# Six PSUM banks for the u blocks, a held exponential and earlier row requests in a fused decoder block

## The chip, the cores and the metric

The kernel is one launch on one core of one Trainium2 chip. The metric is the device time of the launch in microseconds (us); lower is better. Engine names are those of the profile: PE (matmul), DVE (vector), ACT (activation), POOL (issues the indirect DMAs), SP (issues the other DMAs).

## The reference, cut to what matters

A decoder block on 512 tokens of width 1024: adaLN, windowed attention beside a short convolution, an output projection, and then PEER, in which each token takes 8 x 16 of 16384 single-neuron experts. PEER is what the change is about:

```python
vals, ids = top_k(sc, 16)                       # per head, two halves of 128 keys
cand = vals[..., 0, :, None] + vals[..., 1, None, :]
top, pos = top_k(cand, 16)
idx, g = take_along_axis(cid, pos), softmax(top)
# per chunk of 128 tokens:
a   = einsum('chkd,cd->chk', u_tab[idx], x)     # rows of u, dot with the token
out = einsum('chk,chkd->cd', g * gelu(a), v_tab[idx])
```

## The kernel before

Tokens are split. For the first 384 (three chunks, ND = 3) PEER is done densely: every expert's pre-activation is computed by matmul, multiplied by a gate matrix that is zero for experts not chosen, and multiplied with all of v. For the last chunk of 128 tokens, and for the u side of 32 of the others, rows are gathered by indirect DMA and reduced on DVE.

**u blocks.** `first()` (L609) does one of 128 u blocks: `weights_of` loads 512 KB (SP queue, five buffers), splits it into hi (ACT, L176) and lo (DVE, L177), four buffers each; `mm3` runs 24 matmuls of 352 columns into a PSUM tile `pa`; ACT applies Gelu (L621). `pa` comes from pool `psa`, which has two banks; all other PSUM tiles come from `bank()`, pool `psm`, six banks. The first 68 blocks go out to DRAM (`Ad`), the rest stay in a ring.

**Order of the work.** Two u blocks, then the lookup of the dense chunks with three blocks per step (18 in all; from the fourth step also dots of `last_dense`, each held to an earlier block by `held[0]`), then the `ijg` transposes and three blocks, then 24 gate builds. `build(bt)` makes one-hot factors on DVE (x on ACT L919, one buffer, rewritten at every even bt; A L935; B1 and B2 L939; two buffers each), 32 small matmuls `gps` into four banks, and four ACT copies into `st`; every second build stores `st` to `Gd` (L953, SP queue). Two u blocks follow each of builds 0 to 15, one each of builds 16 to 23. Nine u blocks (63 to 71) come after the last build. The dense stage follows: `gated(m)` reads Gd back (`G`, L965) and forms hi and lo weights (L971, L972, L176, L177); `second(j)` runs 18 matmuls of 512 columns into six accumulators, which hold all six banks of `psm` to the end; from j = 68 on, one u block alternates with each `second`.

**The gathered chunk.** `gathered()` (L866) is a generator; its yields are costs, and the loops draw from it until their budget `todo` is used: 2.5 per build, 2.3 per block after the builds, `PACE` per `second`. It routes heads 0 to 3 (`route`: top-k on `scg`, `lookup`, `numbers` writes row numbers `eG`), then alternates dots with the steps of heads 4 to 7. `row(k)` asks for rows up to k + 7 (`fetch`, L770, POOL); before the dense stage the rows share one tag of six buffers. When all 128 dots are done, `weights(1, Rg)` (L697) forms the softmax: DVE subtracts (L701), ACT takes the exponential (L702), DVE sums and divides (L704 to L706). Gelu of the dots and 128 axpys (L905) follow, and `finish` writes the chunk out at the end.

**Who sets the order on an engine.** The framework fixes each engine's queue when the program is built: it plays the program through with its own costs and, when an engine is free, takes the ready instruction that stands first in program order. So later work that is ready early is pulled forward as filling. On the chip each engine runs its queue strictly in that order, and an instruction that is not ready holds all behind it. `after(ins, mark)` adds a dependency on an earlier instruction and so also delays its place. `mark[0]` is the last matmul of the latest `mm3`; `ends` lists such marks per block.

Of the kernel before, what the change touches and what calls it, by code (L numbers as in the profile page):

```python
# [7 lines left out]
F32 = mybir.dt.float32  # L8
# [5 lines left out]
AF = mybir.ActivationFunctionType  # L14
# [4 lines left out]
P = 128  # L19
# [7 lines left out]
TU = TD - HT  # L27
# [8 lines left out]
RING = 3  # L36
LOOK = 3
SPILL = 68
# [3 lines left out]
AHEAD = 7  # L42
# [47 lines left out]
def body(tc, p):  # L90
    nc = tc.nc
    es = ExitStack()

    def pool(name, bufs=1, **kw):
        st = ExitStack()
        return st.enter_context(tc.tile_pool(name=name, bufs=bufs, **kw)), st
# [4 lines left out]
    psa, psa_s = pool("psa", bufs=2, space=PSUM)  # L101
# [8 lines left out]
    def bank(name):  # L110
        return psm.tile([P, 512], F32, tag="m", name=name)
# [55 lines left out]
    mark = [None]  # L167

    def after(ins, mark):

        if mark is not None:
            tc.add_manual_dep(ins.ins, mark.ins.name, mybir.DependencyInfo(
                mybir.DependencyClass.Sync, mybir.DependencyReason.DATA), reason="pace")
# [10 lines left out]
    def parts(src):  # L184

        raw = load(src)
        h = hl.tile([P, D], F32R, tag="h", bufs=4, name="hi")
        l = hl.tile([P, D], F32R, tag="l", bufs=4, name="lo")
        split(h, l, raw)
        return h, l  # L190

    def weights_of(src):

        h, l = parts(src.rearrange("p a b -> p (a b)"))
        return (lambda k: h[:, k * P:(k + 1) * P]), (lambda k: l[:, k * P:(k + 1) * P])

    def mm3(ps, w, rh, rl, ks=range(DC), k0=0, k1=DC - 1):
        wh, wl = w
        for k in ks:
            nc.tensor.matmul(ps, wh(k), rh(k), start=(k == k0), stop=False)  # L200
            nc.tensor.matmul(ps, wh(k), rl(k), start=False, stop=False)  # L201
            mark[0] = nc.tensor.matmul(ps, wl(k), rh(k), start=False, stop=(k == k1))  # L202
# [46 lines left out]
    ps = bank("ss1")  # L249
# [13 lines left out]
    def ada_rows(r):  # L263

        if r % 2 == 0:
            psr[0] = psa.tile([P, 2, 2, P], F32, tag="a", name="psr")
        ps = psr[0][:, r % 2]
        for n in range(2):
            w = load(p["adaR"][r, n].rearrange("p a b -> p (a b)"))
            for i in range(4):  # L270
                kb = 4 * n + i
                nc.tensor.matmul(ps, ccol[:, kb:kb + 1].to_broadcast([P, P]), w[:, i * 256:(i + 1) * 256],
                                 start=(kb == 0), stop=(kb == DC - 1))
        return ps
# [8 lines left out]
    for m, k in enumerate(ORDER):  # L283
        if k < DC - NR:
            ada((k, 8 + k))
        else:
            ps = ada_rows(m)
# [193 lines left out]
    for step in PLAN.split():  # L481
        n = [int(x) for x in step[1:]]
# [80 lines left out]
    h2N = pp.tile([P, D], F32, name="h2N")  # L563
# [41 lines left out]
    Ad = dp.tile([SPILL // 2, P, 2, TU], F32, name="Ad")  # L605
    ring = {}
    lead = [0]

    def first():  # L609
        j = lead[0]  # L610
        if j == NJ:
            return
        lead[0] += 1
        w = weights_of(p["uL"][j])
        ps = psa.tile([P, TU], F32, tag="a", name="pa")
        mm3(ps, w, lambda k: h2H[:, k, :], lambda k: h2L[:, k, :])
        m, i = divmod(j, 2)
        if i == 0:
            ring[m] = up.tile([P, 2, TU], F32, name="sp", bufs=3) if j < SPILL else \
                rg.tile([P, 2, TU], F32, name="ge", bufs=RING)  # L620
        nc.scalar.activation(ring[m][:, i], ps, AF.Gelu_apprx_tanh)  # L621
        if i and j < SPILL:
            nc.sync.dma_start(Ad[m], ring.pop(m))
# [70 lines left out]
                nc.vector.tensor_add(dst[:, c, hs], eq[:, :, 0, :], eq[:, :, 1, :])  # L694
                yield

    def weights(n, R):  # L697
        g = R["g"]
        v = R["v"]
        sh = [P, n, 8, 16]  # L700
        nc.vector.tensor_sub(g, v, v[:, :, :, 0:1].to_broadcast(sh))  # L701
        nc.scalar.activation(g, g, AF.Exp)  # L702
        z = rt.tile([P, n, 8], F32, tag=f"z{n}", name="z", bufs=1)
        nc.vector.reduce_sum(z, g, axis=X)  # L704
        nc.vector.reciprocal(z, z)
        nc.vector.tensor_mul(g, g, z[:, :, :, None].to_broadcast(sh))  # L706
# [41 lines left out]
    last = None  # L748
    for hp in range(16):
# [3 lines left out]
        last = now  # L753
# [16 lines left out]
    def fetch(tab, e):  # L770
        more[0] = bool(more[1]) and not more[0]
        t = more[1][0].tile([P, D], F32, name="row2", bufs=4) if more[0] else r4.tile([P, D], F32, name="row", **R4)
        d = nc.gpsimd.indirect_dma_start(out=t, out_offset=None, in_=tab,  # L773
                                         in_offset=bass.IndirectOffsetOnAxis(ap=e, axis=0))
        if len(done) > 1:
            after(d, done.pop(0))
        return t

    def dot(a, t, h):
        junk = rt.tile([P, D], BF16, name="junk", **R2)  # L780
        return nc.vector.scalar_tensor_tensor(junk, t, 1.0, h, op0=OP.mult, op1=OP.mult, accum_out=a)  # L781

    held = [None]
# [29 lines left out]

    gN = pp.tile([P, P], F32, name="gN")
    ahead = None
    ends = []
    for n, _ in enumerate(lookup(ND, Rd)):
        if n == 1:
            ei = rt.tile([P, P], I32, tag="rest", name="ei", bufs=2)
            numbers(ei, Rd, ND - 1)  # L820
            for q in range(0, P - HT, HT):
                nc.sync.dma_start(eH[q:q + HT, :], ei[P - HT:P, q:q + HT])
            nc.vector.tensor_copy(eH[P - HT:P, :], ei[P - HT:P, P - HT:P])
            nc.vector.tensor_copy(gN, Rd["g"][:, ND - 1].rearrange("p a b -> p (a b)"))
            ahead = last_dense()
        for k in range(LOOK):
            ends.append(mark[0])
            first()
            if n > 2 and k < 2:
                held[0] = ends[-3]  # L830
                next(ahead)
    for c in range(ND):
        pt = bank("ijg")
# [10 lines left out]
        n = P if c < ND - 1 else P - HT  # L844
# [21 lines left out]
    def gathered():  # L866

        Rg = results(1, rg)
        ei = rg.tile([P, P], I32, name="eG")
        av = rg.tile([P, P], F32, name="av")  # L870
        yield from route(Rg, ei, range(0, 4))
        others = route(Rg, ei, range(4, 8))
        vR = p["vL"].rearrange("j i d -> (j i) d")
        rows = []

        def row(k, known=2 * P):

            while len(rows) < min(k + 1 + AHEAD, known):
                q, i = divmod(len(rows), P)
                rows.append(fetch(vR if q else p["uR"], ei[:, i:i + 1]))  # L880
            t, rows[k] = rows[k], None
            return t

        routed = False
        for k in range(P):
            dot(av[:, k:k + 1], row(k, 2 * P if routed else P // 2), h2N)
            yield 1.3
            if not routed:
                x = next(others, None)
                routed = x is None  # L890
                yield x or 0.0
                if k == P // 2 - 1:
                    for x in others:
                        yield x
                    routed = True
        weights(1, Rg)
        nc.scalar.activation(av, av, AF.Gelu_apprx_tanh)
        nc.vector.tensor_mul(av, av, Rg["g"].rearrange("p c a b -> p (c a b)"))
        ga = r4.tile([P, D], F32, name="ga", **R4)
        for k in range(P):  # L900
            t = row(P + k)
            if k == 0:
                nc.vector.tensor_scalar_mul(ga, t, av[:, 0:1])
            else:
                nc.vector.scalar_tensor_tensor(ga, t, av[:, k:k + 1], ga, op0=OP.mult, op1=OP.add)  # L905
            yield 1.3
        total[0] = ga
# [70 lines left out]
    def second(js, ws):  # L978

        ops = [(*w, *parts(p["vL"][j])) for j, w in zip(js, ws)]  # L980
        for c, hf in [(c, hf) for hf in range(2) for c in range(ND)] if len(js) == 1 else \
                [(c, hf) for c in range(ND) for hf in range(2)]:
            cs = slice(c * P, (c + 1) * P)
            hs = slice(hf * 512, hf * 512 + 512)
            for j, (wh, wl, vh, vl) in zip(js, ops):
                if j == 0:
                    acc[c, hf] = bank(f"o{c}{hf}")
                o = acc[c, hf]
                nc.tensor.matmul(o, wh[:, cs], vh[:, hs], start=(j == 0), stop=False)  # L989
                nc.tensor.matmul(o, wh[:, cs], vl[:, hs], start=False, stop=False)  # L990
                last = nc.tensor.matmul(o, wl[:, cs], vh[:, hs], start=False, stop=(j == NJ - 1))  # L991
        done.append(last)
        del done[:-2]

# [14 lines left out]
            nc.sync.dma_start(p["out"][c * P:(c + 1) * P, hs], x1[:, hs])  # L1009

    gb, gb_s = pool("gb")
    total = [None]
    gth = gathered()
    todo = 0.0
    nb = TD // 16
    for bt in range(nb):
# [7 lines left out]
        if not left:  # L1024
            todo += 2.5
            while todo > 0:
                todo -= next(gth)
    for k in range(SPILL + 2 * RING - 2 - lead[0]):
        first()
        todo += 2.3  # L1030
        while todo > 0:
            todo -= next(gth)
# [88 lines left out]
```

## Time and profile before

| what | us |
|---|---|
| times of three runs | 1454.32, 1452.81, 1461.66; median 1454.32 |
| the profiled execution | 1453.08, of which its span is 1451.3 |
| PE busy in the span | 1394.5 (96%) |
| DVE busy in the span | 1240.8 (85%) |
| ACT busy in the span | 616.3 (42%) |
| granted TensorE clock, mean | 0.987 |

The span runs from the first to the last instruction; 1.78 us of the profiled execution lie around it. A granted clock of 1.00 is 2.4 GHz, 0.50 is 1.2 GHz. All positions below are us from the start of the span.

### The profile page before, as it was taken

What the parts mean: (1) busy time and instruction counts of PE and PEld (TensorE: products, weight loads), DVE (VectorE), ACT (ScalarE), POOL (GpSimd) and SP (SyncE); (2) the same over time, 40 slices, a digit from 0 to 9 for tenths busy, and PEclk for the clock granted to TensorE, in tenths of its full rate; (3) what the DMA queues carried; (4) which work ended last, traced back from release to release, by engine and by line L of the source; (5) the groups of instructions that cost most, each with busy time, mean ns of one, the idle gap of its engine ahead of it and who ended that gap; (6) DMA issues with size and microseconds to landing.
All of it is one profiled execution on the core that took longest, in us unless ns stands there. A gap on an engine that the chain in (4) does not pass through costs nothing.

```text
span 1451.3 us, 21225 instructions
## 1 busy us (share of the span) xinstructions
PE 1394.5 (96%) x7696; PEld 1224.8 (84%) x7696; DVE 1240.8 (85%) x2267; ACT 616.3 (42%) x1041; POOL 405.3 (28%) x292
## 2 busy tenths in 40 slices
PE   6999998999898999798999999999999999999998
PEld 4676776788898999798988888889899999999997
DVE  7778977899999999898568888988889898889944
ACT  4524636433634556364433333433343334333431
POOL 0000000000022320511024454446646455555300
PEclk9999999999999999999999999999999999999999
DMA  7645544222586997899989999999999999999843
GB/s 276 225 158 181 194 140 170 85 96 77 176 306 239 372 381 260 309 345 343 326 301 381 401 402 373 405 344 371 341 400 360 387 352 381 386 337 402 295 130 131
DMA packets 134376, 418.80 MB, mean 289 GB/s; under 512 B 12800, under 2 KB 39552, under 8 KB 132736
## 3 DMA queue, kind: packets, MB, share of 16 engines
q1 hardware_dynamic: 92800, 266.45, 51.1%
q0 software_dynamic: 41472, 151.01, 27.5%
q8 instruction: 60, 0.98, 0.3%
q14 instruction: 44, 0.36, 0.1%
HBM read 375.77 MB, written 41.62 MB: 288 GB/s over the span
## 4 chain that ended last, share of the span: by engine, by line
PE 22%; issue 14%; POOL 8%; DMA 7%; DVE 5%; ACT 0%; POOLq 0%; DVEq 0%; ACTq 0%
POOL row L773 8%; DMA row<-in_uR,eG 5%; PE pa L200 4%; PE pa L202 4%; PE pa L201 4%; PE o L990 3%; PE o L991 3%; PE o L989 3%; DMA row<-in_vL,eG 2%; DVE lo L177 2%; DVE junk L781 1%; DVE wwl L177 0%; DVE ga L905 0%; DMA raw<-in_vL 0%; DVE x L1008 0%
## 5 line engine op out<-in xcount | busy, mean ns | idle before, releaser
L176 ACT ACTIVATE hi<-raw 128x1024 fp32r<-128x1024 f32 x298 | 312.2, 1053 | 303.2 <-PE pa L201 83.9
L177 DVE TENSOR_TENSOR lo<-raw,hi 128x1024 fp32r<-128x1024 f32 x298 | 362.4, 1217 | 49.2 <-ACT hi L176 48.7
L200 PE MATMUL pa<-h2H,hi 128*128 128x352 f32 x1024 | 336.1, 328 | 21.1 <-ACT sp L621 21.1
L202 PE MATMUL pa<-h2H,lo 128*128 128x352 f32 x1024 | 332.8, 325 | 0.4 <-DVE lo L177 0.4
L201 PE MATMUL pa<-h2L,hi 128*128 128x352 f32 x1024 | 332.0, 324 | 0.0
L989 PE MATMUL o<-hi,wwh 128*128 128x512 f32 x768 | 299.5, 390 | 0.0
L990 PE MATMUL o<-lo,wwh 128*128 128x512 f32 x768 | 299.1, 389 | 0.2 <-DVE lo L177 0.2
L991 PE MATMUL o<-hi,wwl 128*128 128x512 f32 x768 | 298.9, 389 | 0.3 <-DVE wwl L177 0.3
L773 POOL DMA_INDIRECT row<-in_uR,eG x128 | 188.9, 1476 | 326.1 <-PE o L991 165.7
L781 DVE SCALAR_TENSOR_TENSOR junk<-row,h2N 128x1024 bf16<-128x1024 f32 x128 | 153.9, 1220 | 72.9 <-DMA row<-in_uR,eG 72.7
L200 PEld LDWEIGHTS pa<-h2H,hi 128*128 128x128 f32 x1024 | 194.8, 190 | 25.1 <-ACT sp L621 22.8
L773 POOL DMA_INDIRECT row<-in_vL,eG x128 | 171.7, 1341 | 145.6 <-PE o L991 91.3
L201 PEld LDWEIGHTS pa<-h2L,hi 128*128 128x128 f32 x1024 | 195.3, 191 | 2.2
L202 PEld LDWEIGHTS pa<-h2H,lo 128*128 128x128 f32 x1024 | 195.2, 191 | 0.7 <-DVE lo L177 0.7
L905 DVE SCALAR_TENSOR_TENSOR ga<-row,av,ga 128x1024 f32<-128x1024 f32 x127 | 163.0, 1283 | 25.6 <-DMA row<-in_vL,eG 24.5
L773 POOL DMA_INDIRECT row<-in_uR,eH x32 | 44.5, 1392 | 489.3 <-ACT sp L621 394.8
L991 PEld LDWEIGHTS o<-hi,wwl 128*128 128x128 f32 x768 | 144.1, 188 | 30.9 <-DVE wwl L177 0.7
L990 PEld LDWEIGHTS o<-lo,wwh 128*128 128x128 f32 x768 | 144.2, 188 | 28.7 <-DVE lo L177 0.6
L989 PEld LDWEIGHTS o<-hi,wwh 128*128 128x128 f32 x768 | 144.2, 188 | 28.2 <-issue 0.2
L176 ACT ACTIVATE wwh<-w 128x768 fp32r<-128x768 f32 x64 | 54.1, 845 | 156.9 <-DVE w L972 123.3
L971 ACT ACTIVATE w<-G 128x32 f32<-128x32 f32 x128 | 22.3, 222 | 196.3 <-DVE wwl L177 191.6
L177 DVE TENSOR_TENSOR wwl<-w,wwh 128x768 fp32r<-128x768 f32 x64 | 60.8, 951 | 10.5 <-ACT wwh L176 10.5
(265 smaller groups left out, 1831.2 us busy)
## 6 DMA issues: line engine op xcount, KB each, us to landing
raw<-in_uL SPq DMA_DIRECT2D x128, 512.0 KB, 6.2
raw<-in_vL SPq DMA_DIRECT2D x128, 512.0 KB, 6.9
Gd<-st SPq DMA_DIRECT2D x12, 2048.0 KB, 10.4
G<-Gd SPq DMA_DIRECT2D x16, 1536.0 KB, 11.7
ada<-in_ada SPq DMA_DIRECT2D x32, 512.0 KB, 4.2
Ad<-sp SPq DMA_DIRECT2D x34, 352.0 KB, 6.5
sp<-Ad SPq DMA_DIRECT2D x34, 352.0 KB, 7.1
raw<-in_w_in SPq DMA_DIRECT2D x18, 512.0 KB, 4.9
```

What stands on the lines that cost most here:

```text
L176: nc.scalar.activation(h, f, AF.Copy)
L177: nc.vector.tensor_sub(l, f, h.bitcast(F32))
L200: nc.tensor.matmul(ps, wh(k), rh(k), start=(k == k0), stop=False)
L201: nc.tensor.matmul(ps, wh(k), rl(k), start=False, stop=False)
L202: mark[0] = nc.tensor.matmul(ps, wl(k), rh(k), start=False, stop=(k == k1))
L773: d = nc.gpsimd.indirect_dma_start(out=t, out_offset=None, in_=tab, in_offset=bass.IndirectOffsetOnAxis(ap=e, axis=0))
L781: return nc.vector.scalar_tensor_tensor(junk, t, 1.0, h, op0=OP.mult, op1=OP.mult, accum_out=a)
L905: nc.vector.scalar_tensor_tensor(ga, t, av[:, k:k + 1], ga, op0=OP.mult, op1=OP.add)
L971: nc.scalar.activation(wv[:, i, nu:], g[:, i, nu:], AF.Copy)
L989: nc.tensor.matmul(o, wh[:, cs], vh[:, hs], start=(j == 0), stop=False)
L990: nc.tensor.matmul(o, wh[:, cs], vl[:, hs], start=False, stop=False)
L991: last = nc.tensor.matmul(o, wl[:, cs], vh[:, hs], start=False, stop=(j == NJ - 1))
```

## The change

Four edits. `first()` takes its PSUM tile from `bank()` (six banks by turns) while `free[0]` is true: for blocks 0 to 22 and, after the builds, for blocks 63 to 69; blocks 23 to 62 and from 70 on keep the two banks of `psa`. `ends` is now filled inside `first()`, after the block's matmuls; `ends[-4]` after the block is the mark that `ends[-3]` was, so `held[0]` is unchanged. In `gathered()` seven rows are asked for as soon as the row numbers stand, one step (2.5) is yielded, and the dots of rows 0 to 3 wait for the mark of twelve blocks before. The exponential in `weights(1, Rg)` waits for `mark[0]`, which `second()` now sets too.

```diff
+    ends = []
+    free = [True]
     def first():
...
-        ps = psa.tile([P, TU], F32, tag="a", name="pa")
+        ps = bank("pa")[:, 0:TU] if free[0] else psa.tile([P, TU], F32, tag="a", name="pa")
         mm3(ps, w, lambda k: h2H[:, k, :], lambda k: h2L[:, k, :])
+        ends.append(mark[0])
...
-    def weights(n, R):
+    def weights(n, R, mark=None):
...
-        nc.scalar.activation(g, g, AF.Exp)
+        after(nc.scalar.activation(g, g, AF.Exp), mark)
...
         for k in range(LOOK):
-            ends.append(mark[0])
             first()
             if n > 2 and k < 2:
-                held[0] = ends[-3]
+                held[0] = ends[-4]
...
         routed = False
+        while len(rows) < AHEAD:
+            rows.append(fetch(p["uR"], ei[:, len(rows):len(rows) + 1]))
+        first_row = ends[-12]
+        yield 2.5
         for k in range(P):
-            dot(av[:, k:k + 1], row(k, 2 * P if routed else P // 2), h2N)
+            d = dot(av[:, k:k + 1], row(k, 2 * P if routed else P // 2), h2N)
+            if k < 4:
+                after(d, first_row)
...
-        weights(1, Rg)
+        weights(1, Rg, mark[0])
...
         # second(), after its matmuls
+        mark[0] = last
...
     gb, gb_s = pool("gb")
+    free[0] = False
...
-    for k in range(SPILL + 2 * RING - 2 - lead[0]):
+    more_u = SPILL + 2 * RING - 2 - lead[0]
+    for k in range(more_u):
+        free[0] = k < more_u - 2
         first()
```

## Rows read from the trace of the kernel before

**Rows 1.** The page: busy time of the engines (us, share of the span, instructions).
```profile
PE 1394.5 (96%) x7696; PEld 1224.8 (84%) x7696; DVE 1240.8 (85%) x2267; ACT 616.3 (42%) x1041; POOL 405.3 (28%) x292
```
**Rows 2.** The windows by stage. Columns: stretch and its length, then busy us (and instructions) of PE, PEld, DVE, ACT, POOL, then granted clock, DMA share, GB/s.
```profile
349.00:444.30 95.30, 90.45 (x550) 89.46 (x549) 91.83 (x308) 47.10 (x65) 14.46 (x11) 0.96 0.63 210
444.30:454.40 10.10, 6.11 (x58) 5.74 (x57) 10.10 (x19) 5.87 (x10) 2.08 (x2) 1.00 0.72 240
454.40:608.90 154.50, 152.62 (x1285) 150.08 (x1282) 148.83 (x243) 79.34 (x134) 43.98 (x28) 1.00 0.88 328
608.90:657.80 48.90, 42.05 (x394) 40.88 (x394) 48.90 (x88) 28.68 (x51) 7.13 (x6) 0.93 0.91 326
704.60:1439.00 734.40, 733.41 (x3622) 642.20 (x3621) 602.99 (x660) 271.60 (x423) 332.25 (x239) 1.00 0.93 348
```
**Rows 3.** The waits of PE, whole span: us in total, times, longest.
```profile
PE pa L200 <- ACT sp L621: 21.1, 7, 6.6
```
**Rows 4.** The timeline of PE: the first matmul after each wait in question (start, length; in brackets the idle time before it and what ended it).
```profile
363.82 0.43 PE L200 MATMUL pa<-h2H,hi 128*128 128x352 f32 x1 [1.80 <-ACT sp L621]
...
370.96 0.66 PE L200 MATMUL pa<-h2H,hi 128*128 128x352 f32 x1 [3.05 <-ACT sp L621]
...
446.33 0.43 PE L200 MATMUL pa<-h2H,hi 128*128 128x352 f32 x1 [1.97 <-ACT sp L621]
...
451.56 0.22 PE L947 MATMUL gps<-B,A 128*128 128x128 f16 x1 [1.10 <-DVE B L939]
...
615.57 0.66 PE L200 MATMUL pa<-h2H,hi 128*128 128x352 f32 x1 [6.64 <-ACT sp L621]
...
675.08 0.66 PE L200 MATMUL pa<-h2H,hi 128*128 128x352 f32 x1 [5.79 <-ACT sp L621]
```
**Rows 5.** The windows of four single u blocks, instructions of `pa` alone: stretch and length, PE, PEld and ACT busy, granted clock, DMA. The first is an undisturbed block, the others follow three of the waits.
```profile
427.85:431.87 4.02, 4.02 (x26) 4.02 (x26) 0.45 (x1) 1.00 0.87 294
370.96:377.74 6.78, 6.78 (x26) 6.78 (x26) 0.46 (x1) 0.57 0.60 205
615.57:621.32 5.75, 5.74 (x24) 5.46 (x24) 0.45 (x1) 0.69 0.97 350
675.08:681.71 6.63, 6.63 (x25) 6.63 (x26) 0.45 (x1) 0.58 0.97 316
```
**Rows 6.** The timeline of ACT around the wait at 609.
```profile
613.49 0.73 ACT L919 ACTIVATE x<-slots 128x640 f16<-128x640 f16 x1 [12.56 <-DVE A L935]
...
615.08 0.44 ACT L621 ACTIVATE sp<-pa 128x352 f32<-128x352 f32 x1
```
**Rows 7.** The timeline of DVE, 599 to 614: the dot of row 2, and the A that ACT waits for.
```profile
599.92 1.23 DVE L781 SCALAR_TENSOR_TENSOR junk<-row,h2N 128x1024 bf16<-128x1024 f32 x1 [5.29 <-DMA row<-in_uR,eG]
...
612.18 1.22 DVE L935 TENSOR_TENSOR A<-iota,x 128x2048 f16<-128x2048 f16 x1
```
**Rows 8.** The timeline of POOL: the second and third row request.
```profile
584.14 0.94 POOL L773 DMA_INDIRECT row<-in_uR,eG  x1 [0.30 <-issue]
585.39 6.40 POOL L773 DMA_INDIRECT row<-in_uR,eG  x1 [0.30 <-issue]
```
**Rows 9.** The last build: the timeline of DVE (both B), and of PE (its first `gps`).
```profile
653.50 2.34 DVE L939 TENSOR_TENSOR B<-H,L 128x2048 f16<-128x2048 f16 x2
...
655.56 0.23 PE L947 MATMUL gps<-B,A 128*128 128x128 f16 x1
```
**Rows 10.** The timeline of ACT around the wait at 669.
```profile
664.66 1.28 ACT L702 ACT_TABLE_LOAD   x1
669.09 0.31 ACT L702 ACTIVATE Rg<-Rg 128x128 f32<-128x128 f32 x1 [3.15 <-DVE Rg L701]
672.19 1.06 ACT L668 ACTIVATE ex<-I 128x1024 f16<-128x1024 uint32 x1 [2.79 <-DVE eq L689]
673.26 1.28 ACT L621 ACT_TABLE_LOAD   x1
```
**Rows 11.** The way to block 69: the timeline of SP (the last store of Gd), of POOL (the first row in the new pool), of DVE (its dot, and lo of block 69), of PE (block 69 starts).
```profile
664.75 0.33 SPq L181 DMA_DIRECT2D raw<-in_uL  x1
665.17 0.38 SPq L953 DMA_DIRECT2D Gd<-st  x1
...
676.39 1.65 POOL L773 DMA_INDIRECT row<-in_uR,eG  x1 [12.00 <-DVE eq L692]
...
686.86 1.23 DVE L781 SCALAR_TENSOR_TENSOR junk<-row,h2N 128x1024 bf16<-128x1024 f32 x1 [5.70 <-DMA row<-in_uR,eG]
...
688.01 1.22 DVE L177 TENSOR_TENSOR lo<-raw,hi 128x1024 fp32r<-128x1024 f32 x1
...
693.20 0.32 PE L200 MATMUL pa<-h2H,hi 128*128 128x352 f32 x1
```
**Rows 12.** The end of the dots in the dense stage: the timeline of ACT (Gelu of the dots), of PE (the block after `second(79)`), and of DVE (last axpys, and their first reader).
```profile
1064.01 0.31 ACT L897 ACTIVATE av<-av 128x128 f32<-128x128 f32 x1 [6.29 <-DVE junk L781]
...
1078.70 0.32 PE L200 MATMUL pa<-h2H,hi 128*128 128x352 f32 x1
...
1372.04 2.59 DVE L905 SCALAR_TENSOR_TENSOR ga<-row,av,ga 128x1024 f32<-128x1024 f32 x2
...
1431.24 1.29 DVE L1007 TENSOR_TENSOR fo<-ga,gate 128x512 f32<-128x512 f32 x2
```
**Rows 13.** The groups of instructions of DVE from 589.7 to 655.8, one of them: the dots (count | busy us, mean ns | idle before).
```profile
L781 DVE SCALAR_TENSOR_TENSOR junk<-row,h2N 128x1024 bf16<-128x1024 f32 x9 | 10.9, 1214 | 5.3 <-DMA row<-in_uR,eG 5.3
```

More of the change, by code (lines that the diff above doesn't have):

```diff
@@ L815, in body @@
     ahead = None
-    ends = []
     for n, _ in enumerate(lookup(ND, Rd)):
```

## The prediction, made before the changed kernel ran

> **What bounds the kernel now.** I read the page first, then the windows by stage, then the waits of PE, then the timelines around each wait. PE is busy 1394.5 of 1451.3 us, DVE 1240.8 [rows 1]. From 704.6 to 1439 PE is busy 733.41 of 734.40 us at clock 1.00 [rows 2]: the dense stage is a fixed length that starts when it may, so the time can only change before 704.6 (or by spoiling that stage). The sum is therefore: by how much does the first matmul of the dense stage move? Before it, PE waits seven times for the Gelu of a u block (L621), 21.1 us in all [rows 3]: a block's matmuls need one of two banks, and the Gelu that frees it stands in ACT's queue behind something that waits for DVE. Five of the seven lie where an edit bites: 1.80, 3.05 and 1.97 us around the lookup, 6.64 at 609 and 5.79 at 669 [rows 4]. The other two, 1.85 us together, lie among the builds, where the banks stay as they are. Three of the waits also cost clock. A quiet block takes 4.02 us at 1.00; the blocks that follow the waits of 3.05, 6.64 and 5.79 us take 6.78, 5.75 and 6.63 us at 0.57, 0.69 and 0.58 [rows 5], between the levels of 1.2 and 2.4 GHz: 2.76, 1.73 and 2.61 us more. So the gross prices are: lookup 1.80 + 3.05 + 1.97 + 2.76 = 9.58; 609: 6.64 + 1.73 = 8.37; 669: 5.79 + 2.61 = 8.40. Together 26.35 us.
>
> What the reader should see besides is that DVE is as full as PE there. It is busy 91.83 of 95.3 us, then 10.10 of 10.10, 148.83 of 154.50 and 48.90 of 48.90 up to the end of the builds [rows 2]. A wait of PE that vanishes is only worth what DVE's queue, which keeps its own order, lets PE have.
>
> **Part 1, the wait at 609 (rows asked for early, first dots held).** The chain is: DVE waits 5.29 us for row 2 [rows 7], because its request took 6.40 us on POOL where its neighbour took 0.94 [rows 8]; the A of an odd build therefore starts at 612.18; ACT's next x may only overwrite its one buffer after that A, so it starts at 613.49 after 12.56 us; the Gelu behind it starts at 615.08 [rows 6], and PE at 615.57. The edit issues the same requests at the same point of POOL's queue (before, the first dot asked for eight rows at once; now seven, the eighth with dot 0), so POOL and its order are unchanged. What moves is the dots: one step later in program order, and dots 0 to 3 behind a mark. Counting the generators' yields, the row numbers are written in build 22 after block 61, so `ends[-12]` is block 50. DVE queues its builds in front of the held dots instead of behind them. Bounds: nothing gained if the dots land where they were; 5.29 if the wait is filled; up to 8.37 on PE if some of the 1.2 us dots move behind the builds as well. But from the last build I read a cap: its B run from 653.50 to 655.84 and PE starts on them at 655.56 [rows 9], just in time. So the builds end when DVE lets them, and DVE comes forward by its removed wait: I take 5.3.
>
> By the Trainium skill ("SBUF — State Buffer", section "Who interferes with whom"), descriptors for POOL's DMAs cannot be written while DVE holds a port pair that the two share, but ordinary two-input vector operations are thought not to block that writing. By that rule the 6.40 us would not come from the vector work beside it; the trace here shows the long request and not its cause. If the rule holds, row 2 lands late wherever the dots stand, and the time is that of rival (b), 1449.1; if the vector work was the cause, it may land sooner, and the forecast stands.
>
> **Part 2, the wait at 669 (exponential held, banks for blocks 63 to 69).** The exponential belongs after dot 127, but its input is ready at 669, so it was pulled forward. ACT loads a table (1.28 us), stands until 669.09 for its input, then until 672.19 for `ex`, and loads a table again (1.28) before the Gelu [rows 10]. The hold takes out the exponential and both loads, 2.87 us, but `ex` would still stop ACT until 672.19, so the hold alone brings the Gelu forward only by the second load. The banks do the rest: block 65 no longer needs that Gelu. Together the whole 8.40 can go.
>
> Where the exponential goes: after dot 127 the latest mark is the last matmul of `second(79)`, which ends before 1078.70, against the Gelu of the dots at 1064.01 after 6.29 idle us [rows 12]. Queued behind the waiting exponential on ACT are splits and Gelus of the dense stage; these mostly wait for the same matmuls. The axpys start some 15 us later, plus two loads of 1.28. Their end at 1374.63 has 56.6 us until its first reader at 1431.24 [rows 12]. Cost: 0. If that cover were gone, a late axpy would move the end one for one.
>
> **Part 3, the lookup (banks for blocks 0 to 22).** With six banks PE need not wait for the three late Gelus, so it runs ahead. But the next thing it needs is the first build: `gps` at 451.56 waits for B on DVE [rows 4], and DVE's idle time up to 444.3 is 3.47 us in all, none after that [rows 2]. Whatever PE gains becomes one wait ahead of 451.56. Bounds: +3.5 us if DVE's few idle us also go; -2.8 (the price of a slow block above) if the joined wait drops the clock. I take 0.
>
> **What is late next.** Without parts 1 and 2's stalls PE would reach block 69 13.7 us sooner (5.3 + 8.4), at 679.5. Its lo starts at 688.01, behind a dot that waited 5.70 us for a row [rows 11]. That row is the first to use the memory that the builds give up; its request goes out at 676.39, and the last store of Gd was issued at 665.17, held on SP behind a u load at 664.75 which waits for a buffer that DVE frees [rows 11]. This chain hangs on DVE's end of the builds and comes forward only by part 1's 5.3: lo starts at 682.7 and ends near 683.9. So block 69 starts near 683.9 instead of 679.5: a new wait of 4.4 us.
>
> **Sum.** 5.3 + 8.4 + 0 - 4.4 = 9.3 us off the profiled 1453.08: 1443.8, rounded to 1444. That execution lies 1.24 under the median of the three runs (1454.32), inside their spread, so I don't shift it.
>
> **The rivals.**
> (a) Everything in the two late stalls goes: enough dots leave the builds that DVE is 8.4 ahead, and its dot for the late row stands behind lo of block 69. For it: nine dots of 1.2 us stand before the last B [rows 13], and they are only filling. Against: DVE's queue is full, and the filling that replaces them costs time too. 1453.1 - 8.4 - 8.4 = 1436.3. If the lookup gains its 3.5 as well, 1432.8.
> (b) The rows arrive as late as before and DVE waits for them a little further on, so the builds don't end sooner. Then 669 goes, but lo of block 69 stays where it is, ending near 689.2, against PE's 693.2: 4.0 us, so 1449.1. For it: the 6.40 us request is unchanged. Against: DVE has builds to do in the meantime.
> (c) Slower: the four held dots become ready together and stand one after the other ahead of the last builds' A and B, which have no margin [rows 9]. From the point where DVE's waits there exceed 5.29 + 4.0 us, the kernel is slower than before. Two waits like 5.29 instead of one, four dots (4.9 us) in front of B, and a slow block at 2.8: 1453.1 + 5.3 + 4.9 + 2.8 - 8.4 = 1457.7. For it: requests 2 to 6 all follow the long one. Against: by then the held dots are late in program order, so any ready build goes first.
>
> **How the numbers follow.** Forecast 0.42, (a) 0.27, (b) 0.21, (c) 0.10. The forecast alone covers 1440 to 1448. The range reaches to (a) with part of the lookup and through (b): 1434 to 1452. One per cent is 14.5 us, about what a measurement of this kernel tells from no change: faster by that means under 1438.5, which (a) gives and little else, 0.27; slower by that, over 1467.6, takes (c) with a further stall, 0.03; within it 0.70.
>
> **What would show it.** Right: PE's waits for L621 fall from 21.1 to under 5 us; no wait over 3 us at 609 or 669; no table load between 600 and 700 and two near 1080; PE waits some 6 us or more for B ahead of the first build; a wait of PE for lo (DVE) a few blocks after the builds; DVE's wait for a row near 600 gone. Wrong: a new DVE wait for a row between 595 and 620 (b or c); first `gps` clearly before 449 (the lookup paid after all); PE's order differing, with u blocks in front of the first build; or waits inside the dense stage, which would mean that the held exponential has stopped ACT.

## The result, and the profile after

| | before | after |
|---|---|---|
| median of 8 runs | 1454.55 (1452.81 to 1461.66) | 1446.15 (1439.28 to 1446.75) |
| ratio, 95% interval | | 0.9938 [0.9922, 0.9953] |
| the profiled execution, its span | 1453.08, 1451.3 | 1445.51, 1443.6 |

By the ratio the change is 9.0 us faster (6.8 to 11.3), by the medians 8.4; 9.3 was forecast. Line numbers of the changed kernel are up to 8 higher: L624 is the Gelu (L621 before), L705 the exponential, L776 and L784 row request and dot, L926 `x`, L946 `B`, L954 `gps`.

The page's busy times. Against [rows 1] PE has 2.8 us less of the 7.7 that the span lost, so most of what went is waiting.

```profile
PE 1391.7 (96%) x7696; PEld 1222.1 (85%) x7696; DVE 1242.0 (86%) x2267; ACT 616.1 (43%) x1041; POOL 411.4 (29%) x292
```

The windows by stage, columns as in [rows 2]. DVE is as full up to the end of the builds as it was (155.32 of 155.70, 44.40 of 44.40), and the clock at 610 to 695 is 1.00.

```profile
353.00:454.90 101.90, 90.13 (x563) 89.34 (x562) 97.51 (x314) 49.94 (x68) 16.13 (x13) 0.98 0.65 211
454.90:610.60 155.70, 154.80 (x1281) 152.60 (x1280) 155.32 (x263) 81.20 (x136) 43.35 (x28) 0.98 0.89 329
610.60:655.00 44.40, 42.11 (x418) 40.52 (x417) 44.40 (x67) 28.01 (x50) 8.98 (x6) 1.00 0.94 353
655.00:695.50 40.50, 38.88 (x252) 38.59 (x249) 32.58 (x84) 16.13 (x31) 3.62 (x2) 1.00 0.93 337
695.50:1439.00 743.50, 740.77 (x3654) 648.16 (x3652) 614.42 (x679) 277.02 (x430) 339.16 (x240) 1.00 0.92 348
```

The waits of PE over the whole span. The 21.1 us in 7 waits of [rows 3] are one of 1.4; lo and the first B have taken their place. (Three of the four waits for lo stand in the next timeline; the fourth, 1.69, lies in the dense stage at 1260.92.)

```profile
PE pa L202 <- DVE lo L177: 8.2, 4, 3.2
PE gps L954 <- DVE B L946: 6.9, 1, 6.9
...
PE pa L200 <- ACT sp L624: 1.4, 1, 1.4
```

The timeline of PE: the first u block, the waits that answer to [rows 4], and the first matmul of build 0, of the 17th and the 24th build and of the dense stage.

```profile
352.89 0.41 PE L200 MATMUL pa<-h2H,hi 128*128 128x352 f32 x1
...
374.21 0.43 PE L202 MATMUL pa<-h2H,lo 128*128 128x352 f32 x1 [1.68 <-DVE lo L177]
...
381.50 0.43 PE L202 MATMUL pa<-h2H,lo 128*128 128x352 f32 x1 [3.21 <-DVE lo L177]
...
454.93 0.26 PE L954 MATMUL gps<-B,A 128*128 128x128 f16 x1 [6.92 <-DVE B L946]
...
610.62 0.23 PE L954 MATMUL gps<-B,A 128*128 128x128 f16 x1
...
613.93 0.43 PE L200 MATMUL pa<-h2H,hi 128*128 128x352 f32 x1 [1.35 <-ACT sp L624]
...
653.41 0.23 PE L954 MATMUL gps<-B,A 128*128 128x128 f16 x1
...
684.31 0.42 PE L202 MATMUL pa<-h2H,lo 128*128 128x352 f32 x1 [1.62 <-DVE lo L177]
...
695.54 0.39 PE L996 MATMUL o<-hi,wwh 128*128 128x512 f32 x1
```

The 1.80, 3.05 and 1.97 us of the lookup are 1.68 and 3.21 for lo and one wait of 6.92 for the first B; 6.64 is 1.35; 5.79 is gone and 1.62 for lo of block 69 is new. The timeline of ACT: `x` at the place of [rows 6] idles 7.27 us instead of 12.56; the table loads of [rows 10] stand at 1069.

```profile
611.85 0.74 ACT L926 ACTIVATE x<-slots 128x640 f16<-128x640 f16 x1 [7.27 <-DVE A L942]
...
613.44 0.44 ACT L624 ACTIVATE sp<-pa 128x352 f32<-128x352 f32 x1
...
1055.22 0.31 ACT L904 ACTIVATE av<-av 128x128 f32<-128x128 f32 x1 [5.52 <-DVE junk L784]
...
1069.04 1.28 ACT L705 ACT_TABLE_LOAD   x1
1070.34 0.31 ACT L705 ACTIVATE Rg<-Rg 128x128 f32<-128x128 f32 x1
...
1073.17 1.28 ACT L624 ACT_TABLE_LOAD   x1
```

The timeline of DVE. The first dot no longer comes at 589.7 and none waits near 600 [rows 7]; the row behind the builds is waited for 4.00 us (5.70 in [rows 11]), and lo of block 69 starts at 683.03.

```profile
598.00 1.22 DVE L784 SCALAR_TENSOR_TENSOR junk<-row,h2N 128x1024 bf16<-128x1024 f32 x1
...
680.99 1.23 DVE L784 SCALAR_TENSOR_TENSOR junk<-row,h2N 128x1024 bf16<-128x1024 f32 x1 [4.00 <-DMA row<-in_uR,eG]
...
683.03 2.36 DVE L177 TENSOR_TENSOR lo<-raw,hi 128x1024 fp32r<-128x1024 f32 x2
...
1072.91 0.75 DVE L910 TENSOR_SCALAR ga<-row,av 128x1024 f32<-128x1024 f32 x1
...
1371.33 2.60 DVE L912 SCALAR_TENSOR_TENSOR ga<-row,av,ga 128x1024 f32<-128x1024 f32 x2
...
1423.57 1.29 DVE L1015 TENSOR_TENSOR fo<-ga,gate 128x512 f32<-128x512 f32 x2
```

The timeline of POOL: there still is one long request, now the fourth (5.04 us; the third with 6.40 in [rows 8]), and the row behind the builds is asked for at 672.17. The line of SP is the last store of `Gd`, which stood at 665.17 [rows 11].

```profile
587.79 0.93 POOL L776 DMA_INDIRECT row<-in_uR,eG  x1 [0.30 <-issue]
589.03 5.04 POOL L776 DMA_INDIRECT row<-in_uR,eG  x1 [0.30 <-issue]
...
672.17 1.94 POOL L776 DMA_INDIRECT row<-in_uR,eG  x1 [15.15 <-DVE eq L695]
...
662.53 0.48 SPq L960 DMA_DIRECT2D Gd<-st  x1
```

From first matmuls such as those above, PE's way divides into stages (us). The first column is the start of the first u block, the others lengths, up to the starts of the 17th build, the 24th build, the dense stage, and the end of its last `o`. The experiments are in it already; from e8 on, two u blocks (some 8 us) stand in the second stage instead of the fourth.

| kernel | 1st u block | to 17th build | to 24th build | to dense | dense |
|---|---|---|---|---|---|
| before | 349.3 | 257.7 | 48.6 | 49.1 | 741.9 |
| after | 352.9 | 257.7 | 42.8 | 42.1 | 743.3 |
| e1, no lookup banks | 352.8 | 258.0 | 43.2 | 45.0 | 745.3 |
| e2, lookup banks only | 348.9 | 259.7 | 42.5 | 49.7 | 744.6 |
| e3, rows only | 348.8 | 258.1 | 43.3 | 47.8 | 742.5 |
| e4, hold and end banks | 346.6 | 258.1 | 48.1 | 45.5 | 744.1 |
| e5, hold only | 345.7 | 257.6 | 48.3 | 47.5 | 741.6 |
| e6, end banks only | 347.6 | 259.4 | 47.9 | 44.2 | 745.9 |
| e7, rows without mark | 348.0 | 256.6 | 48.4 | 47.5 | 746.5 |
| e8, five blocks in front | 353.4 | 266.0 | 43.6 | 32.6 | 742.2 |
| e9, and late dots | 348.0 | 266.2 | 39.9 | 32.6 | 745.1 |
| e11, and late routing | 347.3 | 263.5 | 39.9 | 32.6 | 743.6 |
| e12, e11 without lookup banks | 351.1 | 264.1 | 39.7 | 32.4 | 742.8 |
| e13, e11 again | 353.5 | 264.8 | 39.9 | 32.6 | 742.9 |

The change gained 5.8 in the third stage and 7.0 in the fourth, nothing in the second. Its profile lost 3.6 ahead of the first block and 1.4 in the dense stage. These two columns scatter by 8 and 5 us over the kernels, also where no edit touches the code (before and e5: 3.6 apart in the first). The fourth stage scatters too: e1 has the same code there as the change and is 2.9 longer, and e7, whose edit lies earlier, is 1.6 shorter than before. So one profile places a gain and the medians size it.

### The profile page after: what moved, and what is told of

Its sections match the earlier page's. It is cut to its first block, busy times and chain, and to the rows that moved or that the text cites. A ratio compares the mean times of both kernels' runs of the same rounds, so it can differ in the third digit from the quotient of the medians.

```text
span 1443.6 us, 21238 instructions
## 1 busy us (share of the span) xinstructions
PE 1391.7 (96%) x7696; PEld 1222.1 (85%) x7696; DVE 1242.0 (86%) x2267; ACT 616.1 (43%) x1041; POOL 411.4 (29%) x292
## 4 chain that ended last, share of the span: by engine, by line
PE 63%; DVE 24%; DMA 5%; issue 5%; ACT 2%; POOL 1%; SPq 0%; DVEq 0%; ACTq 0%; POOLq 0%
PE o L997 11%; PE o L996 11%; PE o L998 11%; PE pa L200 6%; PE pa L202 6%; PE pa L201 6%; DVE lo L177 4%; DVE junk L213 2%; DVE B L946 2%; DVE junk L784 1%; PE py L200 1%; PE py L201 1%; DVE I L636 1%; PE py L202 1%; POOL row L776 1%
## 5 line engine op out<-in xcount | busy, mean ns | idle before, releaser
L776 POOL DMA_INDIRECT row<-in_uR,eG x128 | 187.4, 1464 | 319.5 <-PE o L998 181.8
L776 POOL DMA_INDIRECT row<-in_vL,eG x128 | 179.8, 1405 | 135.4 <-PE o L998 68.6
L784 DVE SCALAR_TENSOR_TENSOR junk<-row,h2N 128x1024 bf16<-128x1024 f32 x128 | 154.2, 1224 | 63.0 <-DMA row<-in_uR,eG 62.8
L776 POOL DMA_INDIRECT row<-in_uR,eH x32 | 44.0, 1376 | 493.2 <-DVE eq L695 402.9
```

## The experiments

**The lookup banks.** e1 is the change without them, e2 the kernel before with them alone.

```diff
-    free = [True]
+    free = [False]        # e1, in the changed kernel
```

> The changed kernel without its banks for blocks 0 to 22 (two banks there, six for 63 to 69, the rest of the change kept). Theory (the banks of the lookup cost time: PE runs ahead, waits 6.92 us for B of the first build instead of 1.10 and does the blocks behind it at 1.2 GHz): faster than the changed kernel by 2.5 to 6 us, so 1440 to 1444, first gps near 451.5 and no clock drop at 452. Rival (the 3.6 us by which the first u block is later are chance, and the lookup's banks are worth nothing either way): within 1.5 us of the changed kernel, 1445 to 1447.5. Rival 2 (the banks gain there as their gross price says): slower than the changed kernel by 4 to 9 us.

e1: 1446.0 (1440.73 to 1450.88), 0.9925 [0.9904, 0.9946]: the change's time. The theory that the banks cost time fell; the rival, that they are worth nothing, fits.

> The kernel before with six banks for blocks 0 to 22 alone. Theory: no faster, 1 to 6 us slower than before (1455 to 1460), with a wait of 5 to 8 us ahead of the first gps. Rival (no effect): 1453 to 1456. Rival 2 (gross price of the lookup waits is won): 1445 to 1450.

e2: 1455.13 (1446.61 to 1457.34), 0.9996 [0.9981, 1.0011]: no effect. In e1's timeline of PE the three waits for the Gelu are back and the 6.92 is gone:

```profile
367.33 0.43 PE L200 MATMUL pa<-h2H,hi 128*128 128x352 f32 x1 [1.80 <-ACT sp L624]
...
374.47 0.66 PE L200 MATMUL pa<-h2H,hi 128*128 128x352 f32 x1 [3.06 <-ACT sp L624]
...
450.15 0.43 PE L200 MATMUL pa<-h2H,hi 128*128 128x352 f32 x1 [2.25 <-ACT sp L624]
...
455.38 0.22 PE L954 MATMUL gps<-B,A 128*128 128x128 f16 x1 [1.14 <-DVE B L946]
```

Yet the 17th build comes 258.0 us after the first block in e1 and 257.7 in the change: the banks only choose where PE waits for DVE. e2 also showed something not asked for. In its profile the wait at 609 is gone without any edit to the rows (0.17 at 610.72 is left), and POOL's third and fourth request are short there; that the one comes of the other is argued, not tested:

```profile
583.27 0.93 POOL L774 DMA_INDIRECT row<-in_uR,eG  x1 [0.30 <-issue]
584.51 0.94 POOL L774 DMA_INDIRECT row<-in_uR,eG  x1 [0.30 <-issue]
```

**The rows.** e3 is the kernel before with the rows' edit alone; e7 leaves out its mark.

```diff
+        while len(rows) < AHEAD:
+            rows.append(fetch(p["uR"], ei[:, len(rows):len(rows) + 1]))
+        first_row = ends[-12]
+        yield 2.5
...
+            if k < 4:
+                after(d, first_row)      # e3; not in e7
```

> The kernel before with the early row requests and the held dots alone. Theory (the wait at 609 goes with DVE's wait for row 2; from the changed trace 8.3 us between the first and the last build): the wait at 609 falls from 6.64 to under 2 us, the exponential still stops ACT at 669, and lo of block 69 limits what is kept: 4 to 9 us faster than before, 1445 to 1450. Rival (the rows come as late as before, a wait moves): within 1.5 us of before.

e3: 1450.58 (1444.8 to 1454.89), 0.997 [0.9954, 0.9987], that is -4.4. Its third request is still long (5.26 us), so no short request explains this profile. PE's wait at 609 is 1.35, that at 669 stays:

```profile
610.23 0.43 PE L200 MATMUL pa<-h2H,hi 128*128 128x352 f32 x1 [1.35 <-ACT sp L624]
...
669.75 0.66 PE L200 MATMUL pa<-h2H,hi 128*128 128x352 f32 x1 [5.73 <-ACT sp L624]
```

> The kernel before with the rows asked for early and the dots one step later, but with no dot held to a mark. Theory (what helps is that builds stand before the first dots in DVE's queue): one step does not move the dots behind the builds, because they are ready early and are pulled forward; DVE's wait for a row near 600 stays at 3 us or more, PE's wait at 609 too, and the total falls by 0 to 2: about 1453. Rival (one step is enough): the wait at 609 goes to under 2 us and the total falls by 4.4 as with the mark, to 1450.

e7: 1455.18 (1452.35 to 1460.88), 1.0021 [1.0006, 1.0036]. As the theory had it, the dots are pulled forward again: DVE waits for the row, PE for the Gelu.

```profile
596.81 1.23 DVE L784 SCALAR_TENSOR_TENSOR junk<-row,h2N 128x1024 bf16<-128x1024 f32 x1 [4.52 <-DMA row<-in_uR,eG]
```

```profile
612.47 0.66 PE L200 MATMUL pa<-h2H,hi 128*128 128x352 f32 x1 [5.88 <-ACT sp L624]
```

So the early request alone does not do it, and with the mark it does: the intervals of e3 and e7 lie apart. The mark alone was not run. Why e7 is 3.1 us slower than before is open; in its profile the dense stage is 4.6 longer (746.5), while the way to it is no longer than before.

**The exponential and the end banks.** e4 has both on the kernel before, e5 the hold alone, e6 the banks alone.

```diff
-        weights(1, Rg)
+        weights(1, Rg, mark[0])          # e4, e5
...
+        free[0] = k < more_u - 2         # e4, e6; free = [False] at the start
```

> The kernel before with the held exponential and six banks for blocks 63 to 69 alone. Theory: the wait at 669 (5.79) goes, and PE then waits for lo of block 69, which is where it was: 4 us kept of 8.4, 1450 to 1451. Rival (lo of block 69 is no limit): 8.4 us, 1446. Rival 2 (without the rows the dots shift and nothing is won): within 1 us of before.

e4: 1450.16 (1446.46 to 1452.78), 0.9967 [0.9954, 0.9979], -4.8. The wait at 609 stays, 669 is gone, and the new wait for lo at block 69 is there, 3.36 (4.4 by the prediction's working):

```profile
612.75 0.66 PE L200 MATMUL pa<-h2H,hi 128*128 128x352 f32 x1 [6.07 <-ACT sp L624]
...
685.41 0.66 PE L202 MATMUL pa<-h2H,lo 128*128 128x352 f32 x1 [3.36 <-DVE lo L177]
```

> The kernel before with the held exponential alone: no bank is changed, no row is asked for earlier. Theory (the two banks are what stops PE at 669): ACT loses the exponential and both table loads, but `ex` still holds it until about 672.2, so the Gelu comes forward only by the second load, 1.28 us; PE's wait of 5.79 becomes about 4.5 and stays over 3, the total falls by 1.3 at most: about 1453. Rival (the exponential is the cause, the banks are idle): the wait goes as in the kernel with both, the total falls by about 4.8, to 1450.

e5: 1450.41 (1445.84 to 1457.56), 0.9982 [0.9968, 0.9996], -2.6. The timeline of PE, then of ACT:

```profile
669.72 0.43 PE L200 MATMUL pa<-h2H,hi 128*128 128x352 f32 x1 [4.36 <-ACT sp L624]
```

```profile
668.26 1.06 ACT L671 ACTIVATE ex<-I 128x1024 f16<-128x1024 uint32 x1 [7.55 <-DVE l L683]
```

`ex` stops ACT as forecast, and the wait falls by 1.43, near the one load of 1.28. The Trainium skill ("ScalarE: Activation LUTs", section "What ACT_TABLE_LOAD costs") adds a drain of some 1.38 us to a load of 1.283. The load agrees with the 1.28 of [rows 10]; the drain does not show there: `ex` ends at 673.25, the load begins at 673.26.

> The kernel before with the six banks for blocks 63 to 69 alone: the exponential stays where it was, at 669. Theory (the banks do it): PE no longer needs the late Gelu, the wait at 669 is under 1 us, and the block-69 wait for lo of about 3 us takes its place: a fall of about 4.8 as with both, to 1450. Rival (the exponential and its two loads are needed as well, because the hi of a later block stands behind them on ACT): a wait of PE for hi (ACT, L176) of 2 us or more near 675, and less than half of the 4.8.

e6: 1452.21 (1446.39 to 1456.62), 0.9987 [0.9971, 1.0003]. In the trace the banks do all: no wait at 669, though table loads and exponential still stand there, and 3.36 for lo at block 69, as in e4:

```profile
687.78 0.42 PE L202 MATMUL pa<-h2H,lo 128*128 128x352 f32 x1 [3.36 <-DVE lo L177]
```

The stage to the dense one is 4.9 shorter than before, in e5 1.6; but e7, with neither hold nor banks, is 1.6 shorter there as well. The medians do not repeat this order: e5's 1450.41 is nearer to its rival's 1450 than to its theory's 1453, e6's -1.9 is not clear of no change, and the intervals of the two overlap; e6's profile lost 4.0 in the dense stage. Place and mechanism are shown, the share of the total is not. e3 and e4 add up to -9.2 us, the whole change being -9.0. That agrees with two late parts that do not depend on each other, but each of the three numbers is known to some 2 us only.

**What sets the pace.** e8 is the change with five blocks ahead of the first build, to fill PE's wait there.

```diff
-    for k in range(3):
+    for k in range(5):
         first()
     rp_s.close()
```

> The changed kernel with five u blocks instead of three between the lookup and the first build (and so two fewer after the last). Theory (the builds are bound by DVE, and PE's wait of 6.9 us for the first B is idle time that can be filled): PE does the two blocks in that wait, the wait ahead of the first gps falls under 2 us, the builds end when DVE lets them, as in the changed kernel, and the dense stage starts 3 to 6 us earlier: 1440 to 1443. Rival (nothing to gain, because what ends the time before the dense stage is DVE's and SP's chain of the last Gd store, the first lo of the weights, and not PE's work): PE's wait moves behind the builds, the total stays within 1 us of the changed kernel's 1446.

e8: 1442.6 (1440.98 to 1444.7), 0.9922 [0.9905, 0.9939]; the interval overlaps the change's. The 6.92 is gone and PE's waits for the Gelu are 10.2 us in 8, all of them inside the builds. Its windows, builds 1 to 16, 17 to 23, and what follows:

```profile
456.80:619.40 162.60, 153.84 (x1282) 150.61 (x1281) 162.12 (x308) 82.28 (x140) 47.36 (x30) 1.00 0.88 325
619.40:663.00 43.60, 40.55 (x394) 39.02 (x392) 43.60 (x54) 26.45 (x47) 6.62 (x5) 1.00 0.95 363
663.00:695.60 32.60, 32.60 (x226) 32.56 (x225) 21.46 (x46) 15.52 (x28) 0.00 (x0) 1.00 0.88 315
```

DVE is busy 162.12 of 162.60 while PE waits. From the first block to the dense stage it is 342.2 us against the change's 342.6: the wait moved into the builds. The median lies in the theory's range, but a step of the theory failed: the builds were to end as in the change, and the 24th comes 309.6 us after the first block instead of 300.5, with 11 gathered dots of DVE ahead of it instead of nine, so the dense stage starts at 695.61, not 3 to 6 us sooner. The rival looked for the wait behind the builds. The reading that DVE's full queue sets the pace here is made from this trace, and the next two runs test it. In them DVE's filling is taken out of the builds of e8, first the dots (e9), then the routing of heads 4 to 7 too (e11).

```diff
-        first_row = ends[-12]
-        yield 2.5
+        yield 7.5
+        first_row = ends[-1]             # e11: hold[0] = first_row = ends[-1]
...
-            if k < 4:
+            if k < 8:
                 after(d, first_row)
...
-                level1(...)              # in route()
+                level1(..., hold and hold[0])      # e11, heads 4 to 7
```

> The kernel with five u blocks before the builds, and on top of it the dots of the gathered chunk moved behind the builds: three steps later (7.5 instead of 2.5), the first eight held to the last u block instead of four to the one of twelve blocks before. By the queue order DVE has, up to the last B, ten dots of 1.31 us less (with their accumulator reads) and some 3 us more of the routing steps of heads 4 to 7. Theory (with five blocks in front, DVE's queue sets the pace of the builds, and each us of filling taken out of it is a us of PE's wait gone): the last build starts near 653 instead of 663, PE's waits of 10 us inside the builds fall under 3, the dense stage starts at 686 to 689 instead of 695.6: 1433 to 1437. Rival (nothing comes of it, because the dots then stand in front of the lo of the blocks behind the builds and of the first weights): waits of PE for lo between 655 and 700 of 5 us or more, the dense stage starts within 2 us of 695.6: 1441 to 1445.

e9: median 1439.24, 0.9889 [0.9859, 0.992] (one run of 5848.6 is left out of the ratio; the median of the other five is 1438.39).

> As the kernel with five blocks in front and late dots, and the routing steps of heads 4 to 7 are held to the same block behind the builds as well. By the queue order DVE has some 26 us less up to the last B than the kernel with five blocks in front had. Theory (DVE set the pace; with so much room PE does): PE's waits inside the builds fall under 2 us in all, but beyond what the late dots alone give nothing is left, since PE then sets the pace: within 2 us of the kernel with late dots, 1432 to 1437. Rival (the work comes back behind the builds: DVE has over 20 us of filling beside the lo of the last blocks, the first weights and the axpys): it is slower than the kernel with late dots by 3 us or more, by waits of PE for lo between 655 and 800 or by axpys that end after 1400.

e11: 1437.51 (1433.31 to 1438.54), 0.989 [0.9867, 0.9914]. PE's waits for the Gelu, e9, then e11:

```profile
PE pa L200 <- ACT sp L624: 7.2, 5, 2.5
```

```profile
PE pa L200 <- ACT sp L624: 5.3, 3, 2.9
```

First block to dense stage, e8, e9, e11: 342.2, 338.7, 335.9. The direction is the theory's, the size about half of it: e9 was to start the dense stage 7 to 10 us sooner and gained 3.6 on the way to it. Its waits were to fall under 3 us and are 7.2: those of 2.49, 1.90 and 1.64 end before 577, and the first gathered dot that was moved stood at 606.9 in e8. e11's were to fall under 2 and are 5.3, though its time is, as expected, within 2 us of e9's. Both are faster than the change, whose interval theirs do not reach; against e8 the intervals overlap, so there the stages alone speak for it.

**The lookup banks again, now that PE has work in front.** e12 is e11 with two banks for blocks 0 to 22, e13 is e11, on the same chip.

> The kernel with five blocks in front, late dots and held routing, but with the two banks for blocks 0 to 22, as the kernel before has them. Theory (the six banks of the lookup were worth nothing in the change only because the joined wait stood ahead of the first B; now that PE has work to do there, they pay): PE waits for a Gelu at 1.8, 3.0 and 2 us or more ahead of the first build, against 1.5 and 3.15 for lo with six banks, and a slow block: 2 to 5 us slower than the same kernel with six banks, which runs beside it. Rival (they are worth nothing still, since the waits for lo stand where those for the Gelu stood): within 1 us of it.

> The kernel with five blocks in front, late dots and held routing once more, as the comparison for the one without the lookup's banks on the same chip. Expected by both theories: 1433 to 1439, a ratio of 0.987 to 0.991 to the kernel before, no wait of PE over 1 us between the first build and the end of the last one but those of 2.9 and 1.8 that it had.

e12: 1434.71 (1432.73 to 1436.65), 0.9862 [0.9845, 0.988]; e13: 1438.87 (1436.75 to 1440.19), 0.9891 [0.9873, 0.9908]. My theory fell: the six banks do not pay, and without them the kernel is no slower, by the medians 4.2 faster (the intervals overlap a little). The timeline of PE in e12 has its waits ahead of the first build, the largest being

```profile
449.05 0.66 PE L200 MATMUL pa<-h2H,hi 128*128 128x352 f32 x1 [5.58 <-ACT sp L624]
```

and none in the builds: 10.9 us for the Gelu in all. e13 has 5.8 for the Gelu, in the builds, and 4.9 for lo in the lookup: as much, elsewhere. The windows from the first score matmul to the first block, e12, then e13:

```profile
260.63:351.12 90.49, 90.49 (x456) 76.51 (x457) 88.10 (x487) 30.90 (x58) 0.00 (x0) 1.00 0.29 92
```

```profile
261.33:353.51 92.18, 91.67 (x464) 77.48 (x465) 89.78 (x498) 32.15 (x61) 0.00 (x0) 1.00 0.29 93
```

With six banks the last eight score matmuls stand ahead of block 0, after a wait of 0.51. That is all that is fixed in the difference; the rest of the 4.2 is not located. e12 has the lowest median measured: 19 us under the kernel before, 11 under the change.

## Why the prediction was right, point by point

- **Part 1 (5.3 forecast).** Measured: 5.8 in the stage to the 24th build; in e3 5.3 in that stage, and -4.4 in all. The cap was right: DVE still is full up to its last B, and exactly nine dots still stand before it, so only its removed wait was won:

```profile
L784 DVE SCALAR_TENSOR_TENSOR junk<-row,h2N 128x1024 bf16<-128x1024 f32 x9 | 10.8, 1223 | 0.0
```

- **Part 2 and the new wait at block 69 (8.4 - 4.4 = 4.0).** Measured in that stage: 7.0 in the change, 4.1 in e1 with the same code, 3.6 in e4 (-4.8 in all). The 8.4 went; the new wait is the term that was mis-sized: 1.62 in the change, 2.86 in e1, 3.36 in e4. Its chain was right: in the kernel before and in e1 to e7 the row request leaves 0.83 to 0.84 us after the last store of `Gd` has landed. But the forecast took the lengths of these transfers as fixed. From the store's issue to the row request it took 11.22 us before and 9.64 in the change, from the request to the row's dot 10.47 and 8.82, so by these two lo came 3.2 us sooner. Over e1 to e7 the first of these runs from 9.6 to 12.8, also with that code unchanged; why is open. Nor had the forecast priced the clock behind the new wait. In the change it stayed 1.00; in e1 it fell to 0.67 (686.18 to 690.40), and with the wait that is 1.2 longer this makes up the 2.9 by which its stage is longer.
- **The sum.** The dense stage was forecast for 704.64 - 9.3 = 695.3 and started at 695.54. That it is so close is luck: the third and fourth stage gained 12.8 us instead of 9.3, and 3.6 were lost ahead of the first block. The gain of 9.0 over all runs agrees with the forecast, but how long the new wait was in the runs other than the profiled one is not known.
- **Part 3 (0).** Measured: 257.7 and 257.7 us to the 17th build; e1 and e2 show no effect on the time. The forecast joined wait of 6 us or more was 6.92. Its clock cost came, too (0.50 from 454.93 to 459.60), but the 17th build was no later for it, since DVE set its time.
- **The exponential (0).** The loads stand at 1069 and 1073. The dots' Gelu came at 1055.22, 8.8 us sooner with the dense stage; the first axpy came at 1072.91 against 1073.25. The hold thus cost the axpys 8.8 us against the dense stage (15 forecast), and they end at 1373.93, 49.6 before their first reader at 1423.57: hidden, as forecast. PE's waits in the dense stage are 2.6 us, at 1261 and 1266; kernels without the hold have as much there (3.2 in e6, 3.0 in e7).
- **Not foreseen:** the eight score matmuls that moved ahead of block 0 (0.51 of wait, the rest only moved), and how much single profiles scatter. The dense stage, taken as a fixed length, varies by 5 us.
- **The rivals.** (a) would need dots that leave the builds; nine stayed. e9 to e12 take the dots out, and their ways to the dense stage are 4 to 7 us shorter than the change's. (b) and (c) need a late row in front of the last builds; DVE has no wait of 0.1 us or more between 406 and 677. A long request stayed (5.04 us), as (b) had argued, but it ended at 594.07 and the first held dot stands at 598.00. The rule of the Trainium skill on POOL's descriptors ("SBUF — State Buffer", section "Who interferes with whom"), by which ordinary two-input vector operations are thought not to block their writing, is not decided here: the long request of the change lies beside lo, A and B of DVE (588.63 to 593.27), but e2 ran two requests of 1.95 and 1.98 us beside a dot, lo, A and B.

## What to carry to other kernels

When two engines are both full, a wait that is removed on one of them can just move: before counting it, look at whether the other one has idle time in the same stretch (in e8 DVE had almost none, 162.12 busy of 162.60). To gain there, take work off the second engine, or hold its filling until the stretch is over; a bare change of program order did not help (e7), a dependency did (e3). In these traces the extra banks took a wait away where a late result had held others up (the end banks), and only moved it where PE ran ahead to a point that DVE fixed (the lookup banks). And a wait that hangs on transfers should be forecast as a range: the two ahead of block 69's lo were 1.6 us shorter each in the profile of the change than in the one before.

## What the hardware showed that I had not expected

- The clock after a wait is no fixed price. The same wait of 3.2 us in the lookup was followed by clock 1.00 in the change (381.50 to 386.00) and 0.65 in e13 (the window below); 2.49 us in e9 by 0.63, 2.74 in e8, at the same place, by 1.00; 3.36 at block 69 by 0.60 in e4 (685.41 to 689.60) and by 1.00 in e6 (687.78 to 692.00). The prediction took the 2.8 us of a slow block as a bound, and that is all it can be.

```profile
382.12:386.60 4.48, 4.48 (x19) 4.48 (x20) 4.41 (x7) 4.48 (x4) 0.00 (x0) 0.65 0.67 206
```

- An indirect request of 128 rows on POOL took 0.9 to 6.4 us at the same place of the queue. In e2, where the third and fourth were short, PE's wait of 6 us at 609 was gone without an edit there (2.41 us stood 20 us ahead of it instead).
